# S5 Toeplitz tiles taken from on-chip strips, and a new order of the token mixer's steps

## The chip, the cores and the metric

The kernel runs on one core of a Trainium2 chip. The metric is the device time in microseconds of one execution. All tensors are float32; some matmul operands are split into a high and a low part.

## The reference, cut to what matters

256 latent tokens `x` and 256 context tokens `ctx`, width 1024, go through one layer: modulation from `c`, a token mixer of two branches, and a mixture of 32 experts. Only the latent stream is returned.

```python
mod = silu(c) @ w_mod + b_mod;  h, hc = modulated rmsnorm of x and ctx
u, qkv, gate, b_raw, a_raw, br = split(h @ w_in)        # and the same of hc
qkv = silu(short_conv(qkv))                             # 5 taps
ya = s5(u)   # complex diagonal state space, 32 groups x 16 channels x 64 states,
             # two directions, each latent scan starts from the context's last state
ya = gelu(ya) * sigmoid(gelu(ya) @ w_glu + b_glu)
yb = gated_deltanet(l2norm(q), l2norm(k), v, beta, g)   # 4 heads of 128, chunks of 64,
                                                        # a triangular solve in each chunk
yb = rmsnorm(yb) * gdn_norm * silu(gate)
ga, gb = split(sigmoid(br))
x = x + gt1 * ((ga * (ya @ w_branch_a) + gb * (yb @ w_branch_b)) @ w_out)
h2 = modulated rmsnorm of x
x = rmsnorm(x + gt2 * moe(h2))   # top 4 of 32 experts, clamped SwiGLU; each w_gate_up is
                                 # 1024 x 2048, each w_down 1024 x 1024
```

## The kernel before, in words

**Stages.** `front()` loads the inputs, computes the modulation and then runs the steps of the token mixer in the order of the string `ORDER`, followed by the scan of the DeltaNet (`gdn_scan`), `merge` and the experts. A scheduler arranges the instructions of TensorE, ScalarE (ACT), VectorE (DVE) and GpSimd (POOL) by priority, which falls with the place in `ORDER`; `@1000` lowers a step's priority. SyncE's queue (SP) keeps program order and carries all weight loads: `w_in` in tiles of 1 MB (`win`), `w_mod` (`wm`), then 32 experts of 12 tiles. `win` and `wm` go through a ring of five buffers named `ld`; expert weights go through regions of SBUF as the front end frees them.

**Steps.** `k`, `u`, `v`, `q`, `gate`, `br` are projections in chunks of 128 columns. For `q`, `gate` and `br` only latent tokens count, and each weight chunk is first split on chip: the high part is a copy on ACT and the low part a subtraction on DVE (tile `wsp`), then multiplied with `hx`, the split input. `k`, `v`, `q` end in a convolution of five taps (`raw`, `cacc`, `cth`), whose first tap and tanh are on ACT, the rest on DVE. `mod` loads and multiplies one tile of `w_mod`. `proj_ba` makes the DeltaNet's decays (`baT`, later `gsm`).

**S5.** `s5_P` makes tiles P (six products and sums of 128x512 for each of eight half blocks, then transposes on TensorE), `s5_R` tiles R (six such operations for each of four blocks of a direction, from three scaled copies `CC` of the raw weights). `s5_in0`, `s5_in1` multiply the input U with P, `s5_scan` and `s5_steps` run the recurrences, `s5_K` multiplies R with `BB` into strips `KS`. `s5_T` makes the Toeplitz tiles T out of shifted pieces of the strips: `KS` is written to DRAM (`kd`) and read back with a shift. Both transfers stand in ACT's queue. `s5_out` multiplies T with U and R with the states `XL`. `eng()` reads the strings `ENG_P` and `ENG_R`: a V puts a block's operations on DVE and a G on POOL.

**DeltaNet.** `gdn_a` forms the matrix A of all chunks from `kT`, writes it to DRAM (`ad`) and reads it back in another layout as M. The triangular solve (`Y`, L1057 to L1075) is 62 DVE operations on M. The result goes through DRAM (`yd`, `Yb`) to `gdn_b0`.

Names in PSUM are `ps`, all from four pairs of buffers; a chunk can start when a buffer of its pair has been read out.

Of the kernel before, what the change touches and what calls it, by code (L numbers as in the profile page):

```python
# [7 lines left out]
F32 = mybir.dt.float32  # L8
# [3 lines left out]
AF = mybir.ActivationFunctionType  # L12
OP = mybir.AluOpType
# [10 lines left out]
def dram(ap, off, dims):  # L24
    return bass.AP(tensor=ap.tensor, offset=ap.offset + off, ap=dims)


class Kern:
# [114 lines left out]
    def front(self):  # L143
        tc, nc = self.tc, self.nc
        self.smalls()
        self.load_x()
        self.s5_load(0)
        self.mod1()
        self.s5_load(1)
        self.wins, self.winq, self.pair = self.win_order(), [], {}  # L150
        self.ba_load()
        for _ in range(self.WIN0):
            self.win_load()
        self.load_h()
        self.mod1_end()
        self.modulate()
        self.s5_prep()
        self.P = [None, self.s5_P(1)]
        self.P[0] = self.s5_P(0)
        self.s5_C()  # L160
        self.s5_R0()
        step = dict(
            k=self.proj_k(), u=self.proj_u(), v=self.proj_v(), q=self.proj_q(), gate=self.gate(),
            mod=self.mod2(), br=self.br(), ba=self.branch_a())
        for x in self.ORDER.split():
            n, _, times = x.partition("*")
            n, _, pr = n.partition("@")
            for _ in range(int(times or 1)):
                p0 = tc.cur_priority
                if pr:  # L170
                    tc.cur_priority = p0 + int(pr)
                self.rank = tc.cur_priority
                if n in step:
                    next(step[n])()
                else:
                    getattr(self, n)()
                if pr:
                    tc.cur_priority = p0
        self.rank = None
        assert not any([list(x) for x in step.values()])  # L180
        self.gdn_scan()
        tc.cur_priority += 5000
        self.merge()

    ENG_P, ENG_R, ENG_E = "GVGVVGVV", "GGGGGGGG", "VVVV"
    ORDER = """proj_ba u*5 mod*2 gdn_e k mod k mod k mod k mod s5_in0 s5_in1 s5_scan l2k gdn_a s5_R1 s5_steps
        v mod v mod v mod v mod s5_K s5_T lat q mod q mod q mod q mod l2q mod*2 s5_out gdn_b0
        gate@1000*4 br@3000*16 gdn_b1 s5_glu@500 ba@500*8"""

    def mod1(self):  # L190
        nc, I, wk = self.nc, self.I, self.wk
# [254 lines left out]

    def s5_C(self):

        nc = self.nc
        CC = [self.w([128, 32, 16], "CC", "s5") for _ in range(3)]  # L450
        for t, i, x in zip(CC, (2, 2, 3), (1.0, -1.0, -1.0)):
            self.act(t, self.raw[:, i], AF.Copy, scale=x)
        self.CC, self.R = CC, {}

    def s5_R0(self):
        self.s5_R(0, ("XC", "GA"))
# [7 lines left out]

    def s5_R(self, d, reg):

        CC = self.CC
        s0 = 0 if d == 0 else 1
        rr, ri = (self.r(x, f"R{d}") for x in reg)
        vr = rr.rearrange("p (g j c) -> p g j c", g=16, j=8)  # L470
        vi = ri.rearrange("p (g j c) -> p g j c", g=16, j=8)
        for hb in range(4):
            t4 = self.w([128, 4, 8, 16], "rtmp", "g5")
            eng = self.eng(self.ENG_R, 4 * d + hb)
            h = slice(4 * hb, 4 * hb + 4)
            gh = slice(16 * d + 4 * hb, 16 * d + 4 * hb + 4)
            self.tt(vr[:, h], self.bc(CC[0][:, gh]), self.pw(d, 0, s0, hb), OP.mult, eng)
            self.tt(t4, self.bc(CC[2][:, gh]), self.pw(d, 1, s0, hb), OP.mult, eng)
            self.tt(vr[:, h], vr[:, h], t4, OP.add, eng)
            self.tt(vi[:, h], self.bc(CC[2][:, gh]), self.pw(d, 0, s0, hb), OP.mult, eng)  # L480
            self.tt(t4, self.bc(CC[1][:, gh]), self.pw(d, 1, s0, hb), OP.mult, eng)
            self.tt(vi[:, h], vi[:, h], t4, OP.add, eng)
        self.R[d, 0] = rr.rearrange("p (g k) -> p g k", g=16)
        self.R[d, 1] = ri.rearrange("p (g k) -> p g k", g=16)

    def s5_K(self):
        nc, V = self.nc, self.nc.vector


        KS = self.r("H0", "KS")  # L490
        KS = [KS[:, 960 * b:960 * b + 960].rearrange("p (s k) -> p s k", s=4) for b in range(2)]
        dsk = self.w([128, 8], "dsk")
        V.memset(dsk, 0.0)
        for cg in range(4):
            gm = (cg % 2) * 2 + cg // 2
            nc.sync.dma_start(dsk[32 * cg:32 * cg + 16], dram(self.I["s5_d"], gm * 16, [[1, 16], [64, 8]]),
                              allow_slow_non_contiguous=True)
        kd = self.dr.tile([32, 4, 8, 240], F32, name="kd")
        for b in range(2):
            for d in range(2):  # L500
                q = self.pt("s")
                for sl in range(4):
                    slot = 4 * b + sl
                    for c in range(2):
                        for cg in range(4):
                            par, g2 = cg // 2, 2 * slot + cg % 2
                            r = slice(64 * par, 64 * par + 64)

                            m = 32 if c == 0 else 16
                            lw = self.BB[r, 16 * d + g2].rearrange("p x c -> p (x c)")[:, 16 * c:16 * c + m]  # L510
                            self.mm(q[32 * cg:32 * cg + m, 128 * sl:128 * sl + 128], lw, self.R[d, c][r, g2],
                                    start=(c == 0), stop=(c == 1), skip_group_check=True)
                qv = q.rearrange("p (s k) -> p s k", s=4)
                k0 = KS[b][:, :, 112:128]
                if d == 0:
                    self.act(KS[b][:, :, 112:240], qv, AF.Copy)
                    dd = self.w([128, 4, 16], "dd")
                    self.tt(dd, dsk[:, 4 * b:4 * b + 4, None].to_broadcast([128, 4, 16]),
                            self.eye[:, None, :].to_broadcast([128, 4, 16]), OP.mult)
                    self.tt(k0, k0, dd, OP.add)  # L520
                else:
                    self.act(KS[b][:, :, 0:112], qv[:, :, 0:112], AF.Copy)
                    self.tt(k0, k0, qv[:, :, 112:128], OP.add)
            nc.scalar.dma_start(kd[:, :, 4 * b:4 * b + 4].rearrange("h c s k -> c h (s k)"), KS[b].rearrange("p s k -> p (s k)"))
        self.kd_dram = kd

    def bc(self, x):
        return x[:, :, None, :].to_broadcast([128, 4, 8, 16])
# [5 lines left out]
    def s5_P(self, d):  # L534

        nc = self.nc
        s0 = 1 if d == 0 else 0
        dst = [self.r(x, f"P{d}").rearrange("p (g n) -> p g n", g=16) for x in (("PA", "PB") if d == 0 else ("R2", "V"))]
        for hb in range(4):
            gh = slice(16 * d + 4 * hb, 16 * d + 4 * hb + 4)  # L540
            v = [self.w([128, 4, 8, 16], f"pt{i}", "s5") for i in range(3)]
            self.cmul(v[0], v[1], self.bc(self.BB[:, gh, 0]), self.bc(self.BB[:, gh, 1]),
                      self.pw(d, 0, s0, hb), self.pw(d, 1, s0, hb), v[2], self.eng(self.ENG_P, 4 * d + hb))
            for c in range(2):
                q = self.pt("s")
                for i in range(4):
                    self.tr(q[:, 128 * i:128 * i + 128], v[c][:, i].rearrange("p j c -> p (j c)"),
                                        self.ident)
                self.act(dst[c][:, 4 * hb:4 * hb + 4], q.rearrange("p (g n) -> p g n", g=4), AF.Copy)
        return dst  # L550

    def s5_T(self):

        nc, kd = self.nc, self.kd_dram
        self.T = [self.r(x, "T").rearrange("p (g k) -> p g k", g=16) for x in ("H0", "H1")]
        for hf, eng in ((0, nc.scalar), (1, nc.scalar)):
            for j in range(8):
                eng.dma_start(self.T[hf][16 * (7 - j):16 * (7 - j) + 16],
                              dram(kd, 3840 * hf + 16 * (7 - j), [[7680, 16], [240, 16], [1, 128]]))


    def split(self, hi, lo, x):
# [9 lines left out]
    def win_order(self):  # L572

        left = {n: iter([c + x // 2 if x % 2 == 0 else None for x in range(b)]) for n, (c, b) in self.W_IN.items()}
        for x in self.ORDER.split():
            n, _, times = x.partition("*")
# [1205 lines left out]
```

## Time and profile before

| | |
|---|---|
| time, median of 3 runs | 1469.15 us (1466.98 to 1471.56) |
| the profiled execution: its time, its span | 1469.15 us, 1467.4 us |
| mean granted TensorE clock | 0.962 |
| busy: TensorE, DVE, ACT, POOL | 1342.8, 537.1, 249.9, 197.1 us |
| moved by DMA | 474.03 MB, 323 GB/s over the span |

The profiled execution is the median run. Its time is 1.75 us longer than its span. TensorE is the engine with most busy time, but the share over the whole span hides two stages: the token mixer, up to about 502 us, and the experts after it.

### The profile page before, as it was taken

To read this page: it belongs to the slowest core of one execution; us is meant where nothing else is said; L and a number is where in the kernel's file an instruction comes from. 1 tells how busy PE (TensorE), PEld (TensorE's weight loads), DVE (VectorE), ACT (ScalarE), POOL (GpSimd) and SP (SyncE) were. 2 spreads that over 40 slices of the span, in tenths; PEclk is the share of its full clock that TensorE was granted. 3 is DMA by queue.
4 is the path that set the end of the run, shared out by engine and by line. 5 is a ranking of instruction groups with operands and counts; after the bars stand their busy time and mean duration, and the time that the engine had idled before them with its cause. 6 is when DMAs were issued, how large, how long until landed. Compare 5 with 4: busy or idle time off the path is not lost. (4 is left out here: it accounts for less than half of the span.)

```text
span 1467.4 us, 18533 instructions
## 1 busy us (share of the span) xinstructions
PE 1342.8 (92%) x7469; PEld 603.7 (41%) x7469; DVE 537.1 (37%) x1071; ACT 249.9 (17%) x561; POOL 197.1 (13%) x311
## 2 busy tenths in 40 slices
PE   4999964789999899999999999999999999999986
PEld 1344552658878543333333333333333333333321
DVE  4547884765443511222232232232222222222113
ACT  3333221225410110111111111011011110111001
POOL 1358787102000100000000000000000000000000
PEclk9899787889999989999999999999999999999998
DMA  9682029423196989999999999999999999999995
GB/s 330 262 204 101 0 76 245 100 52 115 47 242 239 347 332 389 419 419 419 418 419 419 419 420 418 419 420 418 418 420 419 419 419 419 420 418 420 418 420 202
DMA packets 93282, 474.03 MB, mean 323 GB/s; under 512 B 24664, under 2 KB 28912, under 8 KB 41352
## 3 DMA queue, kind: packets, MB, share of 16 engines
q1 hardware_dynamic: 70912, 460.03, 78.5%
q10 hardware_dynamic: 22280, 12.77, 4.3%
q8 instruction: 61, 1.00, 0.3%
q14 instruction: 29, 0.24, 0.0%
HBM read 468.61 MB, written 4.15 MB: 322 GB/s over the span
## 5 line engine op out<-in xcount | busy, mean ns | idle before, releaser
L79 PE MATMUL ps<-w,xT 128*64 128x512 f32 x2048 | 485.6, 601 | 9.1 <-DMA w<-in_w_gate_up_dram 8.9
L79 PEld LDWEIGHTS ps<-w,xT 128*64 128x64 f32 x2048 | 137.5, 137 | 273.3 <-issue 239.3
L79 PE MATMUL ps<-w,aT 128*64 128x512 f32 x1024 | 233.1, 597 | 11.8 <-DMA w<-in_w_down_dram 11.2
L1718 DVE SCALAR_TENSOR_TENSOR od<-ps,cs,gt 128x512 f32<-128x512 f32 x31 | 23.3, 751 | 469.5 <-PE ps L79 469.5
L79 PEld LDWEIGHTS ps<-w,aT 128*64 128x64 f32 x1024 | 71.5, 137 | 166.5 <-issue 126.7
L94 DVE TENSOR_TENSOR x<-x,ps 128x512 f32<-128x512 f32 x128 | 84.2, 684 | 61.3 <-PE ps L79 61.3
L1499 POOL CAST selsd<-biad 128x128 fp32r<-128x128 f32 x32 | 9.5, 296 | 701.1 <-PE ps L79 701.1
L79 PE MATMUL ps<-hx,wsp 128*128 128x256 f32 (+1 forms) x384 | 82.1, 365 | 22.1 <-ACT wsp L97 18.8
L97 ACT ACTIVATE odh<-od 128x512 fp32r<-128x512 f32 x31 | 19.5, 629 | 427.6 <-DVE od L1718 427.6
L79 PE MATMUL ps<-h,win 128*128 128x512 f32 x192 | 90.3, 617 | 0.0
L79 PEld LDWEIGHTS ps<-hx,wsp 128*128 128x128 f32 x384 | 64.3, 204 | 41.7 <-ACT wsp L97 20.5
L79 PE MATMUL ps<-h,oh 128*64 128x512 f32 x248 | 63.0, 604 | 0.0
L79 PE MATMUL ps<-wm,sc 128*32 128x512 f32 x192 | 31.3, 703 | 28.1 <-DMA wm<-in_w_mod_dram 28.1
L79 PEld LDWEIGHTS ps<-h,win 128*128 128x128 f32 x192 | 36.1, 197 | 48.6 <-issue 44.1
L678 DVE SCALAR_TENSOR_TENSOR cacc<-raw,col_gdn_conv,cacc 128x512 f32<-128x512 f32 (+1 forms) x48 | 46.0, 958 | 7.1 <-ACT cacc L97 6.5
L97 ACT ACTIVATE sgm<-gt 128x512 f32<-128x512 f32 (+1 forms) x33 | 20.3, 618 | 165.6 <-DVE gt L1689 165.6
L94 DVE TENSOR_TENSOR wsp<-win,wsp 128x512 fp32r<-128x512 f32 x48 | 38.1, 818 | 21.8 <-ACT wsp L97 21.8
L1689 DVE TENSOR_SCALAR gt<-ps 128x512 f32<-128x512 f32 (+1 forms) x33 | 22.2, 675 | 58.4 <-PE ps L79 58.4
L97 ACT ACTIVATE aT<-ps 128x512 f32<-128x512 f32 (+1 forms) x33 | 19.3, 584 | 141.4 <-PE ps L83 141.4
L1499 POOL CAST selsg<-biad 128x256 fp32r<-128x256 f32 x32 | 13.9, 435 | 191.7 <-PE ps L79 185.5
L79 PE MATMUL ps<-bias,selsg 128*128 128x512 f32 x64 | 28.7, 474 | 7.2 <-DVE ut L1691 6.3
L79 PE MATMUL ps<-odh,ST 64*128 64x512 f32 x124 | 31.6, 497 | 2.9 <-ACT odh L97 1.6
(359 smaller groups left out, 1436.7 us busy)
## 6 DMA issues: line engine op xcount, KB each, us to landing
w<-in_w_gate_up_dram SPq DMA_DIRECT2D x242, 1024.0 KB
w<-in_w_down_dram SPq DMA_DIRECT2D x121, 1024.0 KB
wm<-in_w_mod_dram SPq DMA_DIRECT2D x24, 1024.0 KB
win<-in_w_in_dram SPq DMA_DIRECT2D x18, 1024.0 KB
w<-in_w_gate_up_dram SPq DMA_DIRECT2D x28, 512.0 KB
w<-in_w_down_dram SPq DMA_DIRECT2D x14, 512.0 KB
wo<-in_w_out_dram SPq DMA_DIRECT2D x4, 1024.0 KB
T<-kd ACTq DMA_DIRECT2D x16, 128.0 KB
```

The lines of the kernel that those rows point to most:

```text
L79: self.last = self.nc.tensor.matmul(out, lhsT, rhs, start=start, stop=stop, **kw)
L94: (eng or self.nc.vector).tensor_tensor(out, a, b, op=op)
L97: self.nc.scalar.activation(out, in_, func, **kw)
L678: nc.vector.scalar_tensor_tensor(acc[:, rows], rt[:, rows, k:k + 64], sc, acc[:, rows], op0=OP.mult, op1=OP.add)
L1499: nc.gpsimd.tensor_copy(v.rearrange("p (n s) -> p n s", s=CAP), dup[:, x:x + n, None].to_broadcast([128, n, CAP]))
L1689: V.tensor_scalar(g, z0, 7.0, None, op0=OP.min)
L1718: V.scalar_tensor_tensor(od, self.pd, self.cs, k.gt2, op0=OP.mult, op1=OP.mult)
```

## The change

Four things are edited. Tiles T are filled by 32 transfers from SBUF to SBUF (64 KB each, 16 partitions), in turn on ACT's and SP's queue; `KS` lies in region PA and the write to DRAM is gone. R of direction 0 is made from the loaded weights, directly after the P tiles' code, so only half-size copies `CC` of direction 1 remain; the imaginary part is a sum that one more ACT operation (128x512) per block negates, eight in all. `s5_P` takes a second set of buffers (`pto`) for every other block, and twelve of its operations move from POOL to DVE. `ORDER` is new: the S5 scan and its inputs stand earlier, `s5_T` stands after two of the four `q`, the four `gate` and two `br` chunks stand ahead of `s5_out` without lowered priority.

```diff
+        self.CC, self.R = [[self.raw[:, i, :16] for i in (2, 3)], None], {}
         self.P = [None, self.s5_P(1)]
         self.P[0] = self.s5_P(0)
+        self.s5_R0()
         self.s5_C()
-        self.s5_R0()
...
-    ENG_P, ENG_R, ENG_E = "GVGVVGVV", "GGGGGGGG", "VVVV"
-    ORDER = """proj_ba u*5 mod*2 gdn_e k mod k mod k mod k mod s5_in0 s5_in1 s5_scan l2k gdn_a s5_R1 s5_steps
-        v mod v mod v mod v mod s5_K s5_T lat q mod q mod q mod q mod l2q mod*2 s5_out gdn_b0
-        gate@1000*4 br@3000*16 gdn_b1 s5_glu@500 ba@500*8"""
+    ENG_P, ENG_R, ENG_E = "VVVVVGVV", "GGGGGGGG", "VVVV"
+    ORDER = """proj_ba u*5 mod*2 gdn_e k mod k s5_in0 s5_in1 mod k mod k s5_scan s5_R1 mod v l2k gdn_a s5_steps
+        mod v mod v mod v mod s5_K lat q mod q s5_T mod q mod q mod l2q mod*2 gate*4 br*2 s5_out gdn_b0
+        br@3000*14 gdn_b1 s5_glu@500 ba@500*8"""
...
-        CC = [self.w([128, 32, 16], "CC", "s5") for _ in range(3)]
-        for t, i, x in zip(CC, (2, 2, 3), (1.0, -1.0, -1.0)):
-            self.act(t, self.raw[:, i], AF.Copy, scale=x)
-        self.CC, self.R = CC, {}
+        CC = [self.w([128, 16, 16], "CC", "s5") for _ in range(2)]
+        for t, i in zip(CC, (2, 3)):
+            self.act(t, self.raw[:, i, 16:], AF.Copy)
+        self.CC[1] = CC
...
+            times(vr[:, h], Cr, 0)
+            times(t4, Ci, 1)
+            self.tt(vr[:, h], vr[:, h], t4, OP.subtract, eng)
+            times(vi[:, h], Ci, 0)
+            times(t4, Cr, 1)
             self.tt(vi[:, h], vi[:, h], t4, OP.add, eng)
+            self.act(vi[:, h], vi[:, h], AF.Copy, scale=-1.0)
...
-        KS = self.r("H0", "KS")
-        KS = [KS[:, 960 * b:960 * b + 960].rearrange("p (s k) -> p s k", s=4) for b in range(2)]
+        KS = self.KS = self.r("PA", "KS")[:, :1920].rearrange("p (s k) -> p s k", s=8)
+        KS = [KS[:, 4 * b:4 * b + 4] for b in range(2)]
...
-            nc.scalar.dma_start(kd[:, :, 4 * b:4 * b + 4].rearrange("h c s k -> c h (s k)"), KS[b].rearrange("p s k -> p (s k)"))
-        self.kd_dram = kd
...
-            v = [self.w([128, 4, 8, 16], f"pt{i}", "s5") for i in range(3)]
+            if hb % 2:
+                v = self.w([128, 2, 4, 8, 16], "pto", "kq")
+                v = [v[:, 0], v[:, 1], self.w([128, 4, 8, 16], "pt2", "s5")]
+            else:
+                v = [self.w([128, 4, 8, 16], f"pt{i}", "s5") for i in range(3)]
...
-        for hf, eng in ((0, nc.scalar), (1, nc.scalar)):
+        for cg in range(4):
             for j in range(8):
-                eng.dma_start(self.T[hf][16 * (7 - j):16 * (7 - j) + 16],
-                              dram(kd, 3840 * hf + 16 * (7 - j), [[7680, 16], [240, 16], [1, 128]]))
+                (nc.scalar, nc.sync)[j % 2].dma_start(
+                    self.T[cg // 2][16 * (7 - j):16 * (7 - j) + 16, 8 * (cg % 2):8 * (cg % 2) + 8],
+                    self.KS[32 * cg:32 * cg + 16, :, 16 * (7 - j):16 * (7 - j) + 128])
```

How the scheduler lays this out is seen in three places. The first is ACT's queue at the second of the four `u` chunks, just after the first read-out of u (`ut`). `P` and `ut` are copies out of PSUM, `R` is the added negation, `us` the DMA that stores u. Before:

```order
L97 ACTIVATE ut<-ps 128x512
L97 ACTIVATE P_376<-ps 128x512
L632 DMA us<-ut 128x512
L97 ACTIVATE P_375<-ps 128x512
L97 ACTIVATE P_376<-ps 128x512
L97 ACTIVATE ut<-ps 128x512
```

And in the changed kernel:

```order
L97 ACTIVATE ut<-ps 128x512
L97 ACTIVATE P_376<-ps 128x512
L639 DMA us<-ut 128x512
L97 ACTIVATE R_544<-R_544 128x512 x2
L97 ACTIVATE baT<-ps 128x512
L97 ACTIVATE ut<-ps 128x512
```

Two negations of R, which follow sums that POOL makes, now stand ahead of the read-out of the `proj_ba` chunk and of the second u chunk.

The second place is ACT's queue from the last strip to the next weight split. Before:

```order
L97 ACTIVATE KS<-ps 128x4x112
L97 ACTIVATE raw_583<-ps 128x4x64
L1059 DMA ad<-At 32x32x32
L97 ACTIVATE wsp<-win 128x512 x2
L1059 DMA ad<-At 32x32x32
...
L97 ACTIVATE cacc<-raw_584,col_gdn_conv 128x256
L1061 DMA M<-ad 128x1024
L97 ACTIVATE raw_583<-ps 128x4x64
L558 DMA T<-kd 16x16x128 x16
L97 ACTIVATE cth<-cacc 128x256
```

And in the changed kernel:

```order
L1066 DMA ad<-At 32x32x32
L97 ACTIVATE KS<-ps 128x4x112
L564 DMA T<-KS 16x8x128
L1068 DMA M<-ad 128x1024
...
L97 ACTIVATE cth<-cacc 128x256
L97 ACTIVATE cacc<-raw_582,col_gdn_conv 128x256
L564 DMA T<-KS 16x8x128 x3
L97 ACTIVATE cth<-cacc 128x256
L564 DMA T<-KS 16x8x128 x8
L97 ACTIVATE wsp<-win 128x512 x2
```

The transfers of T are interleaved with the convolutions of the first two `q` chunks, and the load of M stands ahead of all but one. The last `wsp` row is the split of the third `q` chunk; before, that of the fourth stood ahead of M. The other sixteen transfers stand in SP's queue ahead of the next `wm` and `win` loads.

The third place is DVE's queue around the first operations of the triangular solve (`fst` and `Y`). Before:

```order
L94 TENSOR_TENSOR wsp<-win,wsp 128x512 x2
L683 SCALAR_TENSOR_TENSOR Q<-cth,cacc 128x256
L1064 MEMSET Y 128x1024
...
L94 TENSOR_TENSOR fst<-M,Y 128x31
L94 TENSOR_TENSOR Y<-Y,fst 128x31
```

And in the changed kernel, where 45 rows stand from the first row shown to the one ahead of the first `wsp` row (35 of the solve, 10 of convolutions), and 37 more (27 and 10) from there to the split of the first `gate` chunk, with the splits of two `q` chunks among them:

```order
L94 TENSOR_TENSOR fst<-M,Y 128x31
...
L94 TENSOR_TENSOR Y<-Y,fst 128x15x17
L94 TENSOR_TENSOR fst<-M,Y 128x252
L94 TENSOR_TENSOR wsp<-win,wsp 128x512
L94 TENSOR_TENSOR Y<-Y,fst 128x14x18
```

The low parts of the third and fourth `q` chunk, which stood ahead of the solve, now stand in its middle; before, the first `wsp` row behind the solve's start was that of the first `gate` chunk.

## Rows read from the trace of the kernel before

**Rows 1.** Windows: length, busy PE PEld DVE ACT POOL (x instructions), PEclk, DMA share, GB/s.

```profile
220.00:257.00 37.00, 15.63 (x88) 8.09 (x80) 15.09 (x36) 5.49 (x12) 28.47 (x82) 0.71 0.96 244
257.00:294.00 37.00, 29.58 (x416) 23.70 (x416) 29.08 (x79) 10.41 (x24) 4.97 (x7) 0.83 0.45 104
...
624.00:1430.00 806.00, 778.33 (x3567) 271.49 (x3565) 202.37 (x357) 91.84 (x192) 19.18 (x54) 1.00 1.01 419
```

**Rows 2.** Waits of TensorE from 40 to 502 us: total, times, longest.

```profile
PE ps L79 <- ACT wsp L97: 18.8, 1, 18.8
PE ps L79 <- DMA wm<-in_w_mod_dram: 8.8, 2, 5.8
PE ps L79 <- DVE gsm L1001: 5.5, 1, 5.5
PE ps L83 <- ACT z L97: 5.1, 1, 5.1
PE ps L79 <- DVE KS L94: 3.7, 1, 3.7
PE ps L79 <- ACT raw L97: 3.3, 1, 3.3
PE ps L79 <- DVE kT L94: 2.3, 1, 2.3
```

**Rows 3.** Timeline of DVE, 38 to 68 us: start, length, operation, idle before.

```profile
38.16 0.69 DVE L94 TENSOR_TENSOR bbt<-s5raw,L 128x512 f32<-128x512 f32 x1
...
67.08 1.48 DVE L94 TENSOR_TENSOR pt<-pt,pt 128x512 f32<-128x512 f32 x1
```

**Rows 4.** Timeline of POOL, 36 to 117 us.

```profile
36.40 0.11 POOL L237 MEMSET sc<- 128x8 f32 x1 [18.01 <-PE ps L79]
...
50.17 1.27 POOL L94 TENSOR_TENSOR pt<-pt,pt 128x512 f32<-128x512 f32 x1
...
107.69 1.55 POOL L94 TENSOR_TENSOR R<-CC,PD 128x512 f32<-128x512 f32 x1
```

**Rows 5.** Timeline of ACT, then of TensorE, 65 to 74 us.

```profile
65.92 0.60 ACT L97 ACTIVATE ut<-ps 128x512 f32<-128x512 f32 x1 [1.98 <-PE ps L79]
...
67.68 6.28 PE L79 MATMUL ps<-h,win 128*128 128x512 f32 x14
```

**Rows 6.** Timeline of ACT and its DMA queue (ACTq), 221 to 262 us.

```profile
221.54 3.38 ACTq L1059 DMA_DIRECT2D ad<-At  x1
...
230.65 0.34 ACTq L1061 DMA_DIRECT2D M<-ad  x1
...
238.91 22.59 ACTq L558 DMA_DIRECT2D T<-kd  x16
261.60 0.42 ACT L97 ACTIVATE cth<-cacc 128x256 f32<-128x256 f32 x1 [30.12 <-DMA T<-kd]
```

**Rows 7.** Timeline of DVE, 222 to 266 us.

```profile
222.48 0.21 DVE L94 TENSOR_TENSOR KS<-KS,ps 128x64 f32<-128x64 f32 x1
...
243.78 0.21 DVE L94 TENSOR_TENSOR fst<-M,Y 128x31 f32<-128x31 f32 x1 [9.92 <-DMA M<-ad]
...
248.74 0.38 DVE L94 TENSOR_TENSOR fst<-M,Y 128x192 f32<-128x192 f32 x1
...
263.67 0.68 DVE L94 TENSOR_TENSOR wsp<-win,wsp 128x512 fp32r<-128x512 f32 x1
264.27 0.48 DVE L678 SCALAR_TENSOR_TENSOR cacc<-raw,col_gdn_conv,cacc 128x256 f32<-128x256 f32 x1
264.66 0.68 DVE L94 TENSOR_TENSOR wsp<-win,wsp 128x512 fp32r<-128x512 f32 x1
```

**Rows 8.** Timeline of TensorE, 263 to 276 us.

```profile
263.25 7.94 PE L79 MATMUL ps<-hx,wsp 128*128 128x512 f32 x27 [18.77 <-ACT wsp L97]
...
272.01 0.61 PE L79 MATMUL ps<-T,U 128*32 128x128 f32 x8
...
273.79 1.96 PE L79 MATMUL ps<-T,U 128*32 128x128 f32 x56
```

More of the change, by code (lines that the diff above doesn't have):

```diff
@@ L447, in s5_C @@
     def s5_C(self):
-        nc = self.nc
-        CC = [self.w([128, 32, 16], "CC", "s5") for _ in range(3)]
-        for t, i, x in zip(CC, (2, 2, 3), (1.0, -1.0, -1.0)):
-            self.act(t, self.raw[:, i], AF.Copy, scale=x)
-        self.CC, self.R = CC, {}
+        CC = [self.w([128, 16, 16], "CC", "s5") for _ in range(2)]
+        for t, i in zip(CC, (2, 3)):
+            self.act(t, self.raw[:, i, 16:], AF.Copy)
+        self.CC[1] = CC
     def s5_R0(self):
@@ L465, in s5_R @@
     def s5_R(self, d, reg):
-        CC = self.CC
+        Cr, Ci = self.CC[d]
         s0 = 0 if d == 0 else 1
@@ L475, in s5_R, with times @@
             h = slice(4 * hb, 4 * hb + 4)
[L476 to L481, printed above, removed]
+            def times(out, c, reim):
+                self.tt(out, self.bc(c[:, h]), self.pw(d, reim, s0, hb), OP.mult, eng)
+            times(vr[:, h], Cr, 0)
[3 more added lines that the diff above has]
+            times(t4, Cr, 1)
             self.tt(vi[:, h], vi[:, h], t4, OP.add, eng)
+            self.act(vi[:, h], vi[:, h], AF.Copy, scale=-1.0)
         self.R[d, 0] = rr.rearrange("p (g k) -> p g k", g=16)
@@ L497, in s5_K @@
                               allow_slow_non_contiguous=True)
-        kd = self.dr.tile([32, 4, 8, 240], F32, name="kd")
         for b in range(2):
@@ L552, in s5_T @@
     def s5_T(self):
-        nc, kd = self.nc, self.kd_dram
+        nc = self.nc
         self.T = [self.r(x, "T").rearrange("p (g k) -> p g k", g=16) for x in ("H0", "H1")]
-        for hf, eng in ((0, nc.scalar), (1, nc.scalar)):
+        for cg in range(4):
             for j in range(8):
-                eng.dma_start(self.T[hf][16 * (7 - j):16 * (7 - j) + 16],
-                              dram(kd, 3840 * hf + 16 * (7 - j), [[7680, 16], [240, 16], [1, 128]]))
+                (nc.scalar, nc.sync)[j % 2].dma_start(
+                    self.T[cg // 2][16 * (7 - j):16 * (7 - j) + 16, 8 * (cg % 2):8 * (cg % 2) + 8],
+                    self.KS[32 * cg:32 * cg + 16, :, 16 * (7 - j):16 * (7 - j) + 128])
     def split(self, hi, lo, x):
```

## The prediction

> **What bounds the kernel now.** I read the windows first, to separate the two stages. From 624 to 1430 us [rows 1] the DMA share is 1.01 at 419 GB/s: the experts are paid by their weight stream, whose bytes the change leaves alone. TensorE is busy 778.33 of 806 us there, so it is near that bound and not past it. What the change can move is the moment at which the token mixer hands over. I count a microsecond won or lost in the mixer as one of the whole, because expert weights can only be fetched into regions that the mixer has freed; no row shows this directly.
>
> Inside the mixer TensorE is the engine to follow. The window from 220 to 257 us [rows 1] has it busy for only 15.63 of 37 us, at a clock of 0.71. The waits view [rows 2] names the reason: 18.8 us for a weight split on ACT and 8.8 us for `wm` tiles, 27.6 us in one place, against 5.5 us for `gsm`, 5.1 us for z, and 3.7, 3.3 and 2.3 us (9.3 together) around the strips. The timeline of ACT [rows 6] shows what lies under the large wait. The load of M is issued at 230.65, the sixteen transfers of T occupy the queue from 238.91 for 22.59 us, and the next ACT instruction comes at 261.60 after 30.12 us of idleness. The reader is to see that ACT is not busy then; it is queued behind transfers. But there is a second late thing: DVE could start the triangular solve only at 243.78, after 9.92 us of waiting for M [rows 7].
>
> **The change, by a milestone.** Waits overlap, so I do not subtract 27.6. I follow one event through both kernels: the end of the low part of the first `gate` chunk on DVE, which was at 264.66 + 0.68 = 265.34 [rows 7]. In both orders all `q` chunks and all but at most two `mod` tiles lie ahead of it on TensorE. What TensorE has left after it differs by one thing: T times U, 0.61 + 1.96 = 2.57 us [rows 8], is already done in the new order.
>
> *Step 1, the start.* POOL is free at 36.40 [rows 4] and the R operations need only loaded weights, so they run beside the DVE operations from which the modulation is made. A DVE operation of this size takes 0.69 us, and 1.48 us beside POOL [rows 3]. Four such operations stand there: 4 x 0.79 = 3.2, I take +3. Bounds: 0, if they miss each other, and 6, if the eight scalings behind them stretch by as much again.
>
> *Step 2, the third u chunk.* Two negations stand ahead of two read-outs in ACT's queue (first place in the order rows). They wait for the 24th and 25th operation of POOL. At 1.27 us [rows 4] the 25th ends at 36.5 + 31.8 = 68.3, at 1.55 us [rows 4] at 75.3; I take the middle, 71.8, since DVE is busy for about half of that time. Two negations and one read-out at 0.60 each [rows 5] give 73.6 for the buffer that the third chunk needs, which began at 67.68 [rows 5]. Of the 5.9 us, 3 are those of step 1: +3, bounds 0 and 6.4.
>
> *Step 3.* The decays are now made between the first k chunks, well ahead of their use; the wait of 5.5 for `gsm` [rows 2] goes: -5.5, bound 0.
>
> *Step 4.* R of direction 1 and the scan are both earlier, so the strips' waits of 9.3 [rows 2] shrink. I take two thirds, -6.2 (bounds 0 and -9.3), since `kT` is still scaled by DVE.
>
> The last strip was done at 222.48 + 0.21 = 222.69 [rows 7]; with steps 1 to 4 it is at 222.69 - 5.7 = 217.0.
>
> *Step 5, M.* Before, M was issued 8.0 us after the last strip, 5.7 us after the last issue of `ad` (221.54 + 3.38) [rows 6]. The same transfers stand ahead of it now, so 8.0 stays. It landed 13.1 us after its issue (230.65 to 243.78). For the new landing the nearest rows are 5.7 (the write of the same bytes) and 13.1; I take the middle, 9.4, because fewer weight loads but some T transfers run beside it. M is there at 217.0 + 8.0 + 9.4 = 234.4.
>
> *Step 6, DVE.* The third place in the order rows decides the price. From M on DVE has 35 solve operations and 10 of convolutions ahead of the first split, then 27 and 10 more with 6 split operations up to the milestone. Fifteen solve rows from 243.78 to 248.74 [rows 7] give 0.354 us from start to start; a convolution row 0.39 (264.27 to 264.66), a split row 0.60 (263.67 to 264.27). The first stretch is 12.4 + 3.9 = 16.3, the second 9.6 + 3.9 + 3.6 = 17.1, together 33.4. The milestone is at 267.8, which is 2.5 later than before. So the stall for T is not saved: the solve takes its place, and what steps 3 to 5 give is what keeps this near zero.
>
> *What is costed at nothing.* The transfers of T: if ACT's half still took 22.6 us from the issue of M at 225.0, ACT would be free at 247.6 and the high split done by about 248.8, while DVE reaches the low split at 234.4 + 16.3 = 250.7. The cover is about 2 us; if M came at its lower bound, T would bind instead. SP's half holds back the next `wm` and `win` tiles; the latter is needed some 40 us later. The other six negations, 0.60 each, lie where ACT is busy for 5.49 of 37 us [rows 1]. Twelve operations moved to DVE are 12 x 0.69 = 8.3 us; if DVE had no idle time for them this would be inside the upper bounds of steps 1 and 2.
>
> *Step 7, behind the milestone.* The `gate` and `br` chunks now stand ahead of `s5_out`, so the 5.1 us for z [rows 2] are filled: -5.1, bound 0. The window from 257 to 294 us is at a clock of 0.83 [rows 1], a loss of 0.17 x 37 = 6.3 us; with TensorE fed I take a third back, -2, bounds 0 and -6.3.
>
> Sum: +2.5 - 2.6 - 5.1 - 2 = -7.2. Against the profiled execution, 1469.15 (it is also the median; its span is 1467.4), that is **1462.0**.
>
> **A rule of the notes against the row.** T moved 32 x 64 KB = 2.1 MB in 22.59 us from DRAM [rows 6], 93 GB/s. The Trainium skill ("SBUF — State Buffer", section "Door 1: The DMA port swizzle") says that DMA bandwidth goes by the SBUF ports that the partitions reach, 27.2 GB/s each; sixteen partitions reach four ports, so by an estimate from that page 2.1 MB out of a 16-partition strip take about 19 us, hardly less. That speaks against T being faster from on chip. With 19 or with 22.6 the milestone stays, so the sum is the same by either; it raises the chance of the slow rival below, in which M shares the way with T.
>
> **The rivals.**
>
> *The stall goes entirely.* If splits, solve and transfers interleave without a gap, all 27.6 go: 1441.6. For it: ACT is idle, not busy, and no DRAM trip of the strips is left. Against it: the DVE queue of the new order. Chance 0.15.
>
> *The waits only move (no change).* T is on time, but z, or what follows it, is waited for behind the `br` chunks, and the clock stays: 5.1 + 2 are not given back, and the result is 1469. The rule just named, that T is no faster, leads here as well, since T was hidden either way. Chance 0.23.
>
> *M comes late (slower).* Both queues now carry T around the issue of M. If M lands only with the last of them, 22.6 us after its issue instead of 9.4, the milestone moves by 13.2 and the time is 1475.2. It turns to a loss where M takes over 16.6 us (9.4 + 7.2) and to a measurable one over 21. For it: M took 13.1 when T ran beside it only for the last 4.9. Against it: half of ACT's transfers stand behind M. Chance 0.22.
>
> **Numbers.** The forecast has 0.40. About 0.3%, 4.4 us, is what a measurement of this kernel can tell from no change. The forecast's own bounds, 1455 to 1467, put 0.33 of its 0.40 below 1464.7 and 0.07 within. With the first rival and a little of the second, faster is 0.15 + 0.33 + 0.03 = 0.51; same is 0.07 + 0.17 = 0.24; slower is 0.22 + 0.03 = 0.25. With steps 1 to 5 all at their upper bounds the time would be far above 1475, at their lower bounds near 1445; the range reaches 1443 to 1479, which leaves out the full first rival and the tail of mishaps. The likeliest case alone is 1455 to 1467.
>
> **What the new profile would show.** Step 1: the first h product later than before by about 3 us. Step 2: the third u chunk at about 74 us, with TensorE waiting for ACT. Step 3: no wait for `gsm`. Steps 4 and 5: last strip near 217, M's first use near 234. Step 6: DVE without a gap from there to 268, TensorE waiting for a split on DVE instead of ACT. Step 7: no wait for z. The prediction is wrong if DVE idles between M and the milestone, if the wait for M stays at ten microseconds, or if the mixer ends earlier and the expert stage begins no sooner.

## The result and the profile after

The changed kernel takes 1453.31 us (median of 4, 1450.85 to 1455.58), against 1470.36 for the kernel before (4 runs, 1466.98 to 1474.76): ratio 0.988, 95% interval 0.9857 to 0.9904. It is faster by 17 us, where the forecast had 7. The profiled execution took 1453.78 us, 15.4 less than the one before; its span is 1452.1 us.

I read the same views as before, in the same order. The windows (length, busy PE PEld DVE ACT POOL, PEclk, DMA share, GB/s), which answer to [rows 1]:

```profile
147.00:183.00 36.00, 27.81 (x199) 14.15 (x198) 35.73 (x42) 10.78 (x30) 29.97 (x25) 0.86 0.25 87
183.00:220.00 37.00, 30.30 (x489) 23.25 (x488) 27.09 (x64) 9.33 (x19) 29.70 (x76) 0.95 0.40 81
220.00:257.00 37.00, 18.52 (x157) 12.11 (x160) 27.91 (x75) 5.09 (x11) 18.04 (x51) 0.64 0.69 197
257.00:294.00 37.00, 37.00 (x402) 29.23 (x392) 24.74 (x44) 17.89 (x38) 5.36 (x7) 1.00 0.62 191
294.00:330.00 36.00, 35.73 (x237) 22.58 (x236) 24.00 (x40) 10.57 (x21) 6.62 (x7) 1.00 0.18 59
```

From 257 us on TensorE is full at a clock of 1.00, where it had 29.58 of 37 us at 0.83 [rows 1]. But from 220 to 257 it still stands for half of the time: the hole has become a little smaller and not gone. And from 147 to 183 DVE has no time left (35.73 of 36). The waits of TensorE from 40 to 502 us (total, times, longest), which answer to [rows 2]:

```profile
PE ps L79 <- DMA T<-KS: 25.0, 3, 15.2
PE ps L79 <- ACT sq L97: 8.2, 1, 8.2
PE ps L79 <- DVE h L318: 5.6, 1, 5.6
...
PE ps L83 <- DVE pt L94: 2.6, 1, 2.6
...
PE ps L79 <- POOL rnk L94: 0.2, 1, 0.2
```

The waits for the weight split on ACT, for `wm`, `gsm`, z and the strips are gone. In their place stands T itself, 25.0 us. How the queue of ACT got there, against [rows 6] (start, length; ACTq is its DMA queue):

```profile
205.14 0.93 ACTq L1066 DMA_DIRECT2D ad<-A  x2
...
208.87 0.77 ACTq L564 DMA_DIRECT2D T<-KS  x1
211.77 0.36 ACTq L1068 DMA_DIRECT2D M<-ad  x1
...
224.41 16.28 ACTq L564 DMA_DIRECT2D T<-KS  x8
240.74 0.63 ACT L97 ACTIVATE wsp<-win 128x512 fp32r<-128x512 f32 x1 [15.93 <-DMA T<-KS]
```

DVE, against [rows 7]:

```profile
208.61 0.22 DVE L94 TENSOR_TENSOR KS<-KS,ps 128x64 f32<-128x64 f32 x1 [0.58 <-ACT KS L97]
...
216.63 0.28 DVE L94 TENSOR_TENSOR fst<-M,Y 128x31 f32<-128x31 f32 x1 [2.24 <-DMA M<-ad]
...
234.33 0.42 DVE L94 TENSOR_TENSOR fst<-M,Y 128x252 f32<-128x252 f32 x1
241.40 0.69 DVE L94 TENSOR_TENSOR wsp<-win,wsp 128x512 fp32r<-128x512 f32 x1 [6.65 <-ACT wsp L97]
...
256.55 0.18 DVE L94 TENSOR_TENSOR Y<-Y,fst 128x31 f32<-128x31 f32 x1
...
258.28 0.68 DVE L94 TENSOR_TENSOR wsp<-win,wsp 128x512 fp32r<-128x512 f32 x1
```

And TensorE, whose last row here is the last group of the transposes of x that close the mixer (it stood at 506.94 before):

```profile
44.66 1.89 PE L79 MATMUL ps<-h,wba 128*32 128x512 f32 x2 [5.63 <-DVE h L318]
...
74.94 7.13 PE L79 MATMUL ps<-h,win 128*128 128x512 f32 x16
...
162.32 1.87 PE L79 MATMUL ps<-ones,sq 128*128 128x1 f32 x8 [8.19 <-ACT sq L97]
...
219.99 1.03 PE L79 MATMUL ps<-T,U 128*32 128x128 f32 x4 [6.50 <-DMA T<-KS]
224.33 1.03 PE L79 MATMUL ps<-T,U 128*32 128x128 f32 x4 [3.31 <-DMA T<-KS]
240.53 1.03 PE L79 MATMUL ps<-T,U 128*32 128x128 f32 x4 [15.17 <-DMA T<-KS]
...
489.30 0.63 PE L83 MATMUL ps<-ident,x 128*128 128x128 f32 x4
```

The reader is to see three things. The last strip is done at 208.83, 13.9 us earlier than before [rows 7]. The first operation on M comes 7.8 us after it, where it took 21.1. And then the chain breaks: DVE reaches the split of the third q chunk at 234.75 and idles for 6.65 us, because ACT can't make the high part while eight transfers of T stand in its queue, and TensorE has products T times U at the head of its own queue.

The milestone of the prediction is at 258.28 + 0.68 = 258.96, 6.38 us earlier than before (265.34). From 506.94 to 489.30 are 17.64, so behind the milestone the mixer wins another 11.26. The rest, from that last transpose to the end of the span, is 962.8 us long and was 960.5.

### The profile page after: what moved, and what is told of

Its sections match the earlier page's. It is cut to its first block, busy times and chain, and to the rows that moved or that the text cites. A ratio compares the mean times of both kernels' runs of the same rounds, so it can differ in the third digit from the quotient of the medians.

```text
span 1452.1 us, 18531 instructions
## 1 busy us (share of the span) xinstructions
PE 1338.0 (92%) x7469; PEld 600.9 (41%) x7469; DVE 559.1 (39%) x1083; ACT 255.4 (18%) x568; POOL 179.1 (12%) x299
## 5 line engine op out<-in xcount | busy, mean ns | idle before, releaser
L79 PE MATMUL ps<-w,aT 128*64 128x512 f32 x1024 | 233.1, 597 | 11.4 <-DMA w<-in_w_down_dram 11.1
L94 DVE TENSOR_TENSOR wsp<-win,wsp 128x512 fp32r<-128x512 f32 x48 | 32.0, 701 | 23.8 <-ACT wsp L97 23.5
L685 DVE SCALAR_TENSOR_TENSOR cacc<-raw,col_gdn_conv,cacc 128x512 f32<-128x512 f32 (+1 forms) x48 | 36.3, 756 | 5.5 <-ACT cacc L97 5.3
L97 ACT ACTIVATE wsp<-win 128x512 fp32r<-128x512 f32 x48 | 27.5, 624 | 49.2 <-PE ps L79 27.0
```

Of the source, the lines that this page charges most:

```text
L79: self.last = self.nc.tensor.matmul(out, lhsT, rhs, start=start, stop=stop, **kw)
L94: (eng or self.nc.vector).tensor_tensor(out, a, b, op=op)
L97: self.nc.scalar.activation(out, in_, func, **kw)
L685: nc.vector.scalar_tensor_tensor(acc[:, rows], rt[:, rows, k:k + 64], sc, acc[:, rows], op0=OP.mult, op1=OP.add)
```

## The experiments

Two theories. **Mine:** the gain comes from the early strips, for which the new order and the new preparation of S5 are both needed, and T from on chip takes a part of it back. **The rival:** T without the trip through DRAM is what brings the gain, and the rest only makes room for it. A second question is why M lands so early and T so late. Each run was measured beside the kernel before on the same chip; ratios are to that.

**The new order alone** (before, with the new `ORDER` and nothing else):

```diff
-    ORDER = """proj_ba u*5 mod*2 gdn_e k mod k mod k mod k mod s5_in0 s5_in1 s5_scan l2k gdn_a s5_R1 s5_steps
...
+    ORDER = """proj_ba u*5 mod*2 gdn_e k mod k s5_in0 s5_in1 mod k mod k s5_scan s5_R1 mod v l2k gdn_a s5_steps
...
```

> The kernel before with the new order string alone; strips still go through DRAM, R still comes from the scaled copies. Theory 'order': the new order is what removed the waits around the strips (last strip at 208.8 us instead of 222.7) and let M land 4.9 us after its issue instead of 13.1, so most of the gain of 17 us is here too: 1453 to 1461, with the last strip by about 212 us. Rival 'T on chip': the gain is the missing trip through DRAM, so little is here: 1466 to 1472. Rival 'preparation': R from the loaded weights and the second set of buffers let the scan come early; without them the early scan waits, 1465 or more, with TensorE waiting for P or XC before 150 us.

Measured: 1461.49 us, 0.9936 [0.9912, 0.9959]. Three of TensorE's waits show what the order lacks by itself and what it has:

```profile
PE ps L79 <- ACT wsp L97: 21.1, 1, 21.1
PE ps L79 <- POOL rnk L94: 9.4, 1, 9.4
PE ps L83 <- ACT z L97: 0.3, 1, 0.3
```

POOL is still busy with R and late with the normalised keys (`rnk`), so the last strip comes at 222.4, hardly earlier than before, and the large wait of [rows 2] is still there. So the 9.4 us of this kernel (0.0064 of 1470) do not come from early strips: the wait for z has gone (5.1 before), and that for `wm` has halved (4.5, from 8.8).

**The new preparation alone** (before, with R of direction 0 from the loaded weights, the negation, the second buffers and the twelve operations on DVE):

```diff
-        self.s5_C()
         self.s5_R0()
+        self.s5_C()
...
-    ENG_P, ENG_R, ENG_E = "GVGVVGVV", "GGGGGGGG", "VVVV"
+    ENG_P, ENG_R, ENG_E = "VVVVVGVV", "GGGGGGGG", "VVVV"
```

> The kernel before with the S5 preparation alone (R of direction 0 from the loaded weights, second set of buffers, operations moved from POOL to DVE); old order, T through DRAM. Theory 'POOL early': the preparation matters because POOL has R of direction 0 done by 81 us instead of 140 and so reaches R of direction 1 and the scaling of k sooner; that works with the old order too, so the last strip comes at 212 to 218 us instead of 222.7 and the time is 1458 to 1465. Rival 'only together': with the old order R of direction 1 still waits for the scan's region, strips stay at 221 to 224 and the time at 1466 to 1472.

Measured: 1470.45 us, 0.9997 [0.9976, 1.0017]: nothing. The last strip is at 221.2, 1.5 us earlier than before. DVE, and then the timeline of ACT, which says why nothing follows:

```profile
220.65 0.21 DVE L94 TENSOR_TENSOR fst<-M,Y 128x31 f32<-128x31 f32 x1 [0.45 <-DMA M<-ad]
```

```profile
214.19 0.35 ACTq L1070 DMA_DIRECT2D M<-ad  x1
...
240.14 22.76 ACTq L567 DMA_DIRECT2D T<-kd  x16
262.95 0.42 ACT L97 ACTIVATE cth<-cacc 128x256 f32<-128x256 f32 x1 [31.75 <-DMA T<-kd]
```

M is issued 16.5 us earlier than in [rows 6] and the solve starts 23.1 us earlier than in [rows 7], but T goes out no earlier than there, and ACT is free no earlier.

**Everything but the preparation** (the changed kernel with the old preparation):

```diff
-    ENG_P, ENG_R, ENG_E = "VVVVVGVV", "GGGGGGGG", "VVVV"
+    ENG_P, ENG_R, ENG_E = "GVGVVGVV", "GGGGGGGG", "VVVV"
...
-                v = self.w([128, 2, 4, 8, 16], "pto", "kq")
...
+            v = [self.w([128, 4, 8, 16], f"pt{i}", "s5") for i in range(3)]
```

> The changed kernel with the S5 preparation as before (three scaled copies, R without negation, one set of buffers, POOL taking 12 more operations); order and T on chip stay. Theory 'order': the preparation is worth little, since steps 1 and 2 cost 3.7 and 7 us at the start and the first stage is full either way: 1449 to 1458; the first h product is back near 41 us. Rival 'preparation': P of direction 0 and the scan come later and the gain is lost, 1462 to 1470.

Measured: 1458.14 us, 0.993 [0.991, 0.9949]. The wait for `rnk` is back (9.3 us) and the last strip is at 219.8. Beside the order alone, T on chip made no measurable difference here. Against the changed kernel, the preparation brings the last strip 11.0 us forward but the time only 7 us (0.0050 of 1470).

**Everything but T on chip** (the changed kernel, strips written to DRAM and T read back on ACT's queue, as before; the strips stay in region PA):

```diff
+            nc.scalar.dma_start(kd[:, :, 4 * b:4 * b + 4].rearrange("h c s k -> c h (s k)"), KS[b].rearrange("p s k -> p (s k)"))
...
-                (nc.scalar, nc.sync)[j % 2].dma_start(
-                    self.T[cg // 2][16 * (7 - j):16 * (7 - j) + 16, 8 * (cg % 2):8 * (cg % 2) + 8],
...
+                eng.dma_start(self.T[hf][16 * (7 - j):16 * (7 - j) + 16],
+                              dram(kd, 3840 * hf + 16 * (7 - j), [[7680, 16], [240, 16], [1, 128]]))
```

> The changed kernel with the strips written to DRAM and T read back from there on ACT's queue, as before; all else changed. Theory 'order': the on-chip transfers are no faster (they took 31.7 us from first issue to the last landing, against 22.6 for the sixteen from DRAM), so the time moves by at most 6 us either way: 1449 to 1459. Rival 'T on chip': the gain goes, 1464 to 1472. Rival 'preparation': 1453, no change.

Measured: 1446.09 us, 0.984 [0.982, 0.9861], 5.9 us (0.004 of 1470) better than the changed kernel. The two intervals just touch, but the slowest of its four runs (1448.03) is faster than the fastest of the changed kernel (1450.85); no version that leaves nothing out was faster. Its TensorE:

```profile
219.20 4.38 PE L79 MATMUL ps<-hx,wsp 128*128 128x512 f32 x16 [2.97 <-DVE raw L94]
225.15 1.06 PE L79 MATMUL ps<-wm,sc 128*32 128x512 f32 x8 [1.57 <-DMA wm<-in_w_mod_dram]
238.22 2.08 PE L79 MATMUL ps<-hx,wsp 128*128 128x512 f32 x4 [12.01 <-ACT wsp L97]
246.10 2.78 PE L79 MATMUL ps<-T,U 128*32 128x128 f32 x42 [2.12 <-DMA T<-kd]
```

These waits sum to 18.7 us, against 25.0 for T above: the third q chunk runs before T is there, in place of waiting behind products that need T. And its DVE:

```profile
229.55 0.30 DVE L94 TENSOR_TENSOR fst<-M,Y 128x31 f32<-128x31 f32 x1
...
283.85 0.19 DVE L94 TENSOR_TENSOR Y<-Y,fst 128x31 f32<-128x31 f32 x1
```

The first operation on M comes 12.9 us later than in the changed kernel (DVE did not wait for M itself there) and the solve ends 27.3 us later, and still this kernel is the faster one. So neither M nor the solve was what bound. The rival falls here: the gain is there without T on chip, and in this order, with the reads on ACT's queue, T on chip is a loss. Two experiments below, with T in another place and on another queue, limit this to the present place and queue. With T by DRAM in all three, the ratios give in us of 1470: order alone -9.4, preparation alone -0.4, both -23.5. The last strip is at 222.4, 221.2 and 212.4: only the two together move it by more than 2 us, and what they bring beyond the sum of the two, some 14 us, goes with it. No experiment moves the strip alone.

**No transfers of T** (T is set to zero on POOL):

```diff
-        for cg in range(4):
-            for j in range(8):
-                (nc.scalar, nc.sync)[j % 2].dma_start(
...
+        for t in self.T:
+            nc.gpsimd.memset(t, 0.0)
```

> The changed kernel without any transfer of T: the two tiles are set to zero on POOL instead (the Toeplitz part of the result is left out). It prices T. Theory 'T binds': TensorE's 25 us of waiting for T and ACT's 15.9 us behind its transfers go, the solve binds next, and the time is 1436 to 1446. Rival 'solve binds': DVE's solve holds the splits anyway, as the prediction's step 6 had it: 1449 to 1455.

Measured: 1438.86 us, 0.9791 [0.9758, 0.9824]. By the ratios the transfers of T cost the changed kernel 0.0089 of 1470, 13 us. One window of it:

```profile
220.00:257.00 37.00, 27.55 (x249) 19.82 (x245) 29.75 (x67) 10.52 (x25) 25.36 (x55) 0.77 0.46 179
```

TensorE has 9.0 us more in the hole. The splits of both last q chunks lie at 212 to 221 us here, among the first operations of the solve on DVE, which ends only at 275.9. Again the solve isn't the bound.

**T behind all four q** (on chip, one place in `ORDER` later), and the same with T by DRAM:

```diff
-        mod v mod v mod v mod s5_K lat q mod q s5_T mod q mod q mod l2q mod*2 gate*4 br*2 s5_out gdn_b0
+        mod v mod v mod v mod s5_K lat q mod q mod q mod q s5_T mod l2q mod*2 gate*4 br*2 s5_out gdn_b0
```

> The changed kernel with one move in the order string: s5_T behind all four q chunks instead of behind two. On ACT the splits of the third and fourth q chunk then stand ahead of nearly all T transfers. Theory 'ACT's queue': TensorE gets its third and fourth q chunk before 225 us, its wait for T shrinks to 10 to 15 us, and the time is 1440 to 1448. Rival: T lands as late as now and TensorE only waits in another place: 1451 to 1456.

> The same move with T through DRAM: the fastest kernel so far (1446) with s5_T behind all four q chunks. Theory 'ACT's queue': the 12 us that TensorE waits for the third q chunk's split shrink to under 4, and the time is 1438 to 1445. Rival: M, which takes 12 us beside the strips' write, holds DVE and so the low splits: 1444 to 1449.

Measured: on chip 1448.78 us, 0.9857 [0.9825, 0.9889]; by DRAM 1459.7 us, 0.9944 [0.9905, 0.9983]. On chip the splits come at 212 to 217 us and TensorE's wait for T shrinks from 25.0 to 2.8 us:

```profile
PE ps L79 <- DMA T<-KS: 2.8, 2, 2.6
```

The profiled execution of it is 5.3 us below its median, and its interval overlaps that of the changed kernel, so a gain from this step is likely and not settled. With T by DRAM the same move loses 15 us: the weight split on ACT is waited for twice (14.6 us), the solve ends at 285.4 and z comes at 292.2. Where T stands can't be judged apart from how it travels. The best of each way, 0.984 by DRAM and 0.9857 on chip, can't be told apart.

**How T travels on chip.** Three variants of the 32 transfers. Side by side: those out of partitions below 64 on ACT's queue, those from 64 on on SP's, pieces of both in turn. Then all on SP, and all on ACT:

```diff
-        for cg in range(4):
-            for j in range(8):
-                (nc.scalar, nc.sync)[j % 2].dma_start(
+        for j in range(8):
+            for cg in (0, 2, 1, 3):
+                (nc.scalar, nc.sync)[cg // 2].dma_start(
```
```diff
+                nc.sync.dma_start(
```
```diff
+                nc.scalar.dma_start(
```

> The changed kernel with the 32 transfers in another order: for each shift, strips of partitions 0 to 47 on ACT's queue and of partitions 64 to 111 on SP's, side by side, where the changed kernel takes all of the lower half first. Theory 'ports': the transfers are held by the way out of the sixteen source partitions (about 90 GB/s in the windows before the weight load joins); with both halves in flight T lands by about 226 instead of 240, TensorE's wait for T falls from 25 to under 12 us, and the time by 4 to 12 us: 1441 to 1449. Rival 'pieces': the cost is by piece of 512 bytes or by issue and the same in any order: 1450 to 1456, T's landing within 2 us of 240.

> The changed kernel with all 32 transfers of T on SP's queue, none on ACT's. Theory 'queue': what T on chip costs is ACT's queue, in which the split of the third q chunk (240.7 us) stands behind the last T; with ACT free that split is done before 225, and if the transfers go at about 1 us each as SP's did, T lands near 241 as now, but only the product T times U waits for it: 1441 to 1449. Rival 'pieces': the pieces themselves are slow, TensorE stands at T times U until 240 in any case: 1451 to 1457.

> The changed kernel with all 32 transfers on ACT's queue, none on SP's. Theory 'SP as a gate': M landed 4.9 us after its issue because SP stood behind the strips with its sixteen T transfers and no weight tile was moving; with SP free, weight loads run again, M takes 10 to 14 us, the split of the third q chunk comes later than 240, and the time is 1455 to 1465. Rival 'no gate': M takes 5 to 6 us as in the changed kernel.

Measured: side by side 1455.45 us, 0.9898 [0.9872, 0.9925]; all on SP 1453.9 us, 0.9884 [0.9856, 0.9911]; all on ACT 1454.65 us, 0.9882 [0.9852, 0.9912]. None differs from the changed kernel. With all on SP:

```profile
208.33 25.84 SPq L564 DMA_DIRECT2D T<-KS  x32
234.22 0.69 SPq L216 DMA_DIRECT2D wm<-in_w_mod_dram  x1
```

ACT is free there, and TensorE still waits 14.9 us for T and 6.2 for ACT. Waits only change their name, so ACT's blocked queue is not the cause by itself. With all on ACT the first operation on M comes 4.8 us after its issue, just as with half of T on SP. That run by itself tests little, since SP sent only one weight tile between 191.6 and 231.6 (at 208.66). But in the kernel without transfers of T weight tiles go out at 208.43 and from 212.39 on, the DMA moves 341 GB/s from 210.5 to 215, and the first operation on M comes 4.6 us after its issue too. So SP's holding back of weight loads is not what makes M quick.

The Trainium skill ("SBUF — State Buffer", section "Can I just issue two DMAs to hit both halves?") says that two DMAs at once, one on a tile at partition 0 and one on a tile at partition 64, were only 6% faster than one. The trace agrees: side by side the first product with T stands at 241.24, after a wait of 27.4 us. This doesn't show what the bound is: both queues write, shift by shift, into the same sixteen partitions of the two tiles of T, so the edit spreads the way out and not the way in.

**T by DRAM on SP's queue** (as in "Everything but T on chip", with SP in place of ACT):

```diff
-        for hf, eng in ((0, nc.scalar), (1, nc.scalar)):
+        for hf, eng in ((0, nc.sync), (1, nc.sync)):
```

> The changed kernel with the strips through DRAM and the sixteen reads of T on SP's queue. Theory 'SP as a gate' and 'queue' together: SP waits for the strips' write and so holds the weight loads back, M lands in 5 to 7 us, ACT has nothing to stand behind, T comes within about 15 us of its first issue: 1438 to 1446, faster than with the reads on ACT's queue (1446). Rival: the weight tiles that SP then holds back (four of w_mod and one of w_in) are late for q and gate, and the time is 1446 to 1454.

Measured: 1458.41 us, 0.9928 [0.9902, 0.9953], slower than either forecast and 13 us behind the same transfers on ACT. TensorE waits 26.4 us for T. M was issued at 211.77, as in the changed kernel, and used at 221.43, 9.7 us later:

```profile
221.43 0.20 DVE L94 TENSOR_TENSOR fst<-M,Y 128x31 f32<-128x31 f32 x1 [6.13 <-DMA M<-ad]
```

The strips' write to DRAM was issued 1.8 us ahead of it on the same queue, which the changed kernel doesn't have, and no weight tile was issued between 187.6 and 232.3. In the other kernels with such a write ahead, 5 to 6 us before M, where DVE waited for M, its first use came 13.1 us after the issue (the kernel before) and 6.5 us (the preparation alone). In the six without that write where DVE waited for M, it came after 4.3 to 5.6 us. That the write delays M fits all nine; it was not tried by itself.

**Gate late** (the changed kernel, `gate` and `br` at their old place and priority):

```diff
-        mod v mod v mod v mod s5_K lat q mod q s5_T mod q mod q mod l2q mod*2 gate*4 br*2 s5_out gdn_b0
-        br@3000*14 gdn_b1 s5_glu@500 ba@500*8"""
+        mod v mod v mod v mod s5_K lat q mod q s5_T mod q mod q mod l2q mod*2 s5_out gdn_b0
+        gate@1000*4 br@3000*16 gdn_b1 s5_glu@500 ba@500*8"""
```

> The changed kernel with the gate and br chunks back at lowered priority behind s5_out and gdn_b0. Theory 'step 7': the new place of these chunks fills the wait for z and keeps TensorE's clock at full speed from 257 to 330 us; without it 5 us of waiting for z and some 2 to 4 us of clock come back, 1458 to 1464. Rival: the solve ends 35 us earlier than before, so z and what follows it are ready anyway: 1450 to 1457.

Measured: 1455.01 us, 0.9903 [0.9867, 0.9938], no loss that can be told. z is made at 267.79 and nobody waits for it; the solve ends at 251.6. So the place of `gate` isn't needed for the wait of 5.1 us for z [rows 2] to go when the solve ends early. The new order suffices without an early solve as well: with the order alone the solve ended at 293.2, later than before, and the wait for z was 0.3 us.

## Where the prediction failed and where it held

| step | predicted | measured |
|---|---|---|
| 1, first h product | +3 | +3.7 (44.66, from 40.94) |
| 2, third u chunk | 73.6 to 74 | 74.94 |
| 3, wait for `gsm` | gone | gone |
| 4, last strip | 217.0 | 208.83 |
| 5, M issued behind the strip; landed | 8.0; 9.4 | 2.9; 4.9 at most |
| 6, M to the low split of the third q | 16.3 | 18.1 and then 6.65 idle |
| 6, from there to the milestone | 17.1 | 17.6 |
| milestone | 267.8 | 258.96 |
| 7, behind the milestone | -9.7 | -11.3 |

Two steps failed. Step 4 was mis-sized: it brought the last strip to 217.0, and it was done at 208.83. Step 6 had the wrong path: it let the solve on DVE set the milestone, and what set it was T, which the prediction costed at nothing and whose transfers cost 13 us. Step 5 was mis-sized too, by 9.6 us, but on the path through M that did not bind. That the milestone missed its forecast by only 8.8 us with M 17.8 us early is luck: the wait for T gave the rest back.

The account closes: the milestone moved by -6.4 and not by +2.5, what follows by -11.3 and not by -9.7, and what comes after the mixer took 2.3 longer: together -15.4, the difference of the two profiled executions, where the forecast had -7.2.

**Steps 1 to 3** held in size. Eight scalings of h took 8.94 us on DVE beside POOL, and TensorE waited 5.6 us for them; I had the cause, and took the middle of it. In step 2 the number held and the reason did not: ACT idled 5.9 us for POOL ahead of the first negation, as foreseen, but TensorE didn't wait for ACT, since `mod` and P work filled the time. It waited 2.6 us for a P operation of DVE (`pt`), which took 1.75 us beside POOL.

**Step 4 was mis-sized.** I took two thirds of the strips' waits, with all of them (-9.3) as the bound, and let the second half of the strips keep its pace. The last strip moved by -13.9: +4.8 up to the first product of R, -16.5 in the stretch of these products (189.06 to 207.19, instead of 184.25 to 218.85), and -2.2 behind it. In that stretch TensorE waited 11.1 us before, the three waits of [rows 2] and one more, and 0.2 now:

```profile
PE ps L79 <- ACT KS L97: 1.8, 1, 1.8
```

So the waits went whole. Another 2.8 us of products of the first q chunk left the stretch, and the other 2.7 fit the granted clock, 0.95 instead of 0.82 from 183 to 220. With R of direction 0 on chip at 80.8 instead of 140 us, POOL is free for the DeltaNet's keys. The two experiments without the preparation show what that is worth: 9.3 and 9.4 us of waiting for `rnk`, 0.2 with it. One cost was not foreseen: DVE is full from 147 to 183, and TensorE waits 8.2 us for the squares of k. This wait stands in every kernel with the new order and the new preparation and in none with only one of them. The convolutions' operations on DVE take 1.58 to 1.75 us there, beside R of direction 1 on POOL, and 0.74 with the order alone, where POOL stood still at that time.

**Step 5 was mis-sized.** Both halves came from [rows 6], where the last issue of `ad` took 3.38 us and M stood behind it. Here the issues took 0.93 (two), 0.33 and 0.31 us. M was issued 5.6 us behind the strips' write when its landing took 13.1 us; the changed kernel lacks that write, and the prediction did not price it. Together 9.6 us earlier than I had it.

**Step 6 failed by its bound.** It priced the operations of DVE well, but said that the solve takes the place of the stall for T. M came 17.8 us earlier than predicted, so the cover of 2 us over T, which the prediction named as what would give way, was gone: T bound. DVE idled 6.65 us between M and the milestone, one of the prediction's own signs of being wrong. Two experiments go further: with the solve ending at 284.0 and 275.9 instead of 256.7 the kernel was faster, so the solve did not bind at all in this order. T "costed at nothing" costs 13 us.

**Step 7** nearly has the sum, and its reason is one of two that suffice. The timeline of ACT in the kernel before, which I hadn't followed that far, shows z behind the transfers of the solve's result:

```profile
292.02 0.36 ACTq L1073 DMA_DIRECT2D yd<-Y  x1
294.70 2.21 ACTq L1155 DMA_DIRECT2D Yb<-yd  x4
...
298.24 1.09 ACT L97 ACTIVATE z<-ps 128x512 f32<-128x512 f32 x2
```

The solve ended at 292.0 there. With the solve at 251.6 and the gate chunks at their old place z wasn't waited for either; so the early solve is enough to remove that wait, as is the new order, with `gate` early, without it (0.3 us, with the solve ending at 293.2). The clock gave more than the third that I took: 1.00 instead of 0.83 from 257 to 294.

The rivals: the stall went neither entirely nor not at all; of the slow one (M comes late) the opposite happened. The rule that T is no faster from on chip held, and more than that: from the first issue at 208.87 to the third product's release at 240.53 are 31.7 us. The same stretch, up to the last product that waited for T, took 20.7 us with T by DRAM on ACT's queue (225.38 to 246.10) and 19.7 on SP's.

What stands open: why 2.1 MB of T in 512-byte pieces take so long on chip. From the first issue to the end of the last one are 25.8 us with all on SP and 26.0 with all on ACT, where weight tiles go out only behind them, and 22.3 with the old preparation, where they do so from 239.2. They are 31.8 in the changed kernel and 30.7 side by side, where they go out beside T from 224.8 and 224.7. So the longest times stand where weight loads run beside T; whether these are the cause, and what bounds the rest, no row shows.

## What to carry to other kernels

A milestone on one engine is only as good as the claim that this engine binds: write down by how much each of the others misses it, and what an earlier input would do to that. When a shared engine (POOL here) serves two chains, freeing it in one place can be worth more at the other, and only in an order that puts the other chain early: the two parts were worth 9.4 and 0.4 us apart and 23.5 together, with T by DRAM. Moving transfers on chip is no gain by itself; ask first what stands in each queue behind the operation that needs them.

## What the runs showed of the hardware

Transfers from SBUF to SBUF between 16 partitions were slow. In the first microseconds of T, with the load of M beside them only from 211.77 on, and later:

```profile
209.00:213.00 4.00, 4.00 (x27) 2.67 (x26) 0.96 (x3) 0.39 (x1) 3.61 (x12) 1.00 0.69 87
...
229.00:233.00 4.00, 0.00 (x0) 0.00 (x0) 3.69 (x10) 0.00 (x0) 3.61 (x10) 0.50 1.02 346
```

The DMA engines are 0.69 busy and move 87 GB/s; later, with weight loads beside T, 346 GB/s at 1.02. All 32 on one queue need 25.8 us, 81 GB/s. The Trainium skill ("DMA: Bandwidth & Descriptors", section "Why small descriptors are slow (HBM only)") says that transfers between SBUFs don't suffer the penalty that small descriptors have. No run here moves larger pieces on chip, so this is not tested; with pieces of 512 bytes the issues of T took 22.3 to 31.8 us on chip, and 22.6 us from DRAM in the kernel before [rows 6].

The second row also shows the clock: while TensorE stands still from 229 to 233 the granted clock is at 0.50, the lower of its two levels (1.2 GHz); it is back at 1.00 from 257 on, when TensorE has work without a gap.

The same load of 0.5 MB (M) was waited for until 4.3 to 5.6 us after its issue in the six kernels without a write of the strips to DRAM ahead of it, five of them with transfers of T from SBUF to SBUF beside it, and until 6.5, 9.7 and 13.1 us in three with that write. And from the end of the mixer on, the time hardly depends on what came before: 960.5 us in the kernel before, 962.1 to 965.2 in the changed kernel and the experiments, so a microsecond of the mixer counts as one.
